# Order of emission: steps of the other small-matmul streams wait for the next step of the RWKV7 recurrence and go right behind it

## The chip, the cores and the metric

The kernel runs on one core of one Trainium2 chip (TensorE, VectorE, ScalarE, GpSimd, and SyncE, which issues most of the DMAs). The metric is the device time of one execution in microseconds (us); the time of a kernel is the median of its runs. In the profile the engines are called PE (matmul), PEld (weight load of the PE), DVE (VectorE), ACT (ScalarE), POOL (GpSimd) and SP (SyncE).

## What is computed

Two blocks of two layers each, on 256 tokens with 1024 features, all in float32. The change lies in the first block. Each of its two layers projects the normed input to 18688 columns and runs three mixers on them:

```python
proj = h @ w_in[l]                                     # 1024 -> 18688, 73 chunks of 256 columns
y_a = hgrn2_mixer(a_q, a_ff, a_fb, a_i, ...) * silu(a_g)    # gated linear recurrence, two directions
y_b = retention_mixer(b_q, b_k, b_v, ...) * silu(b_g)       # retention, two directions
y_c = rwkv7_mixer(c_s, mu, ...) * silu(c_g)                 # RWKV7 recurrence, two directions
mixed = gates[0]*(y_a @ w_branch_a) + gates[1]*(y_b @ w_branch_b) + gates[2]*(y_c @ w_branch_c)
x = x + mixed @ w_out[l]
```

The second block (feed-forward, short convolution, latent attention) follows and is not touched.

## The kernel before

**Large matmuls.** Every dense product is done with three TensorE passes: weight and activation are each split into a high and a low float32r part (`split`, L386 on ScalarE and L387 on VectorE or GpSimd), and `mm3` (L345, L346, L347) multiplies low by high, high by low and high by high, each with 128 x 128 weights and 256 moving columns. A chunk of 256 output columns is 16 such steps, 48 matmuls. Weights come as 512 KB loads from the SP queue into `raw` and are split in halves into `whi` and `wlo`.

**Small matmuls.** The mixers work in float32 on pieces of 32 to 128 rows, in PE tiles written in the profile as 32*32, 64*64, 64*128 or 128*32. The RWKV7 recurrence treats eight pairs of heads one after the other. Its matmuls, all in `rwkv_states`, write `psc` (L967), `pb` (L975), `prv` (L984), `pt` (L992), `pw` and `px` (L1018, L1026, and L1041, L1047), `ch` (L1065, L1072, L1081) and `po` (L1099, L1106). The HGRN2 heads write `ppc` (L1227, L1257), `ppt` (L1265, L1271) and `hpo` (L1181); the retention heads `rps` (L1335) and `rpo` (L1346); the preparation of the recurrence's operands `pv` (L877) and `pl` (L891, L892); column sums and their spreading over a tile stand in helpers (L405, L445, L453).

**Streams.** Inside a layer five Python generators emit this work: `recurrences`, `heads` (four pairs of HGRN2 heads, then four of retention heads), `outs`, `operands`, and `weights`, which emits the large matmuls. A generator runs to its next `yield`. A small stream yields its step's planned TensorE time and the planned time until its next step can start, both in ns; `weights` yields 320 after each three-matmul step; a function that is yielded means "wait until this holds" (mostly an event in `ev`, such as a buffer of the ring of five `hj` tiles having been used). `recurrences` yields gaps of 1000 to 2500, for example

```python
            yield 1740, 1200
            tt(W, pw, C["mw"][:, L].unsqueeze(2).to_broadcast([128, 2, 4, 32]), ALU.mult)
```

and `heads`, for each of five levels of a head, `yield 0, 3000` (elementwise work alone) and `yield 440, 0` (its matmuls).

**What sets the order.** `weave` walks a planned clock. At each turn it takes the first small stream, in the order recurrences, heads, outs, operands, that is due by that clock; if none is, the next step of `weights` goes; if `weights` waits, the earliest of the others goes. The planned gap is stretched by 1.3 for recurrences and outs, 1.35 for heads and 0.8 for operands. So `weave` only decides the order in which instructions are emitted. The framework then places them on each engine by that order and by what is ready, and lets the instructions of the recurrence on VectorE, ScalarE and GpSimd move ahead by a fixed number of places (`Ahead`). No wait of the hardware comes from `weave` itself; an engine executes its queue in order, and waits come from data and from buffers.

When `weights` finds that a ring buffer is not yet free, it first emits other large work that needs none (`spare`: gate chunks of the first two branches, or the next r, k, v, g chunk of the recurrence), and then waits.

Of the kernel before, what the change touches and what calls it, by code (L numbers as in the profile page):

```python
# [19 lines left out]
EC = math.exp(-0.5)  # L20
SH = 20.0
NEG = -1e30
RING, NB = 5, 4


# [13 lines left out]
def weave(chains, fill):  # L39

    scale = dict(chains)
    now, ready, wait, live = 0.0, {}, {}, list(scale) + [fill]
    while live:
        free = []
        for g in live:
            if g in wait and wait[g]():
                del wait[g]
                ready[g] = max(now, ready.get(g, 0.0))  # L50
            if g not in wait:
                free.append(g)
        g = next((g for g in free if g is not fill and ready.get(g, 0.0) <= now), None)
        if g is None:
            g = fill if fill in free else min(free, key=lambda g: ready.get(g, 0.0))
        now = max(now, ready.get(g, 0.0))
        v = next(g, None)
        if v is None:
            live.remove(g)
        elif callable(v):  # L60
            wait[g] = v
        elif g is fill:
            now += v
        else:
            now += v[0]
            ready[g] = now + scale[g] * v[1]


# [93 lines left out]
def consts_second():  # L162
# [7 lines left out]
    i = np.arange(128)  # L170
    caus = np.where(i[:, None] >= i[None, :], 0.0, NEG)
    mask = np.concatenate([caus, np.zeros((128, 128)), caus], 1)
# [324 lines left out]
class First(Core):  # L497
# [73 lines left out]
    def layer(s, l, then):  # L571
# [223 lines left out]
        if l == 0:  # L795
            nc.sync.dma_start(out=s.c1, in_=s.a["c1"])
        weave(((recurrences(), 1.3), (heads(), 1.35), (outs(), 1.3), (operands(), 0.8)), weights())
        run(out_c(0))
        run(out_c(1))
# [1034 lines left out]
```

## Time and profile before

| | us |
|---|---|
| median of 3 runs | 2808.9 |
| lowest and highest run | 2807.0, 2813.6 |
| the profiled execution, whole | 2819.4 |
| its span, first to last instruction | 2817.6 |
| PE busy in the span | 2662.0 (94%) |
| DVE busy in the span | 1946.3 (69%) |

The profiled execution is 10.5 us (0.4%) above the median, and 1.8 us of it lie outside its span. The two layers of the first block run from about 40 to 840 us and from 920 to 1720 us; the second block follows to the end. In a timeline of PE each row is a run of equal instructions with its start and its duration. Large matmuls overlap: a new one starts about every 0.12 us, though each is shown with 0.28 us, so starts are to be compared, not durations.

### The profile page before, as it was taken

What the parts mean: (1) busy time and instruction counts of PE and PEld (TensorE: products, weight loads), DVE (VectorE), ACT (ScalarE), POOL (GpSimd) and SP (SyncE); (2) the same over time, 40 slices, a digit from 0 to 9 for tenths busy, and PEclk for the clock granted to TensorE, in tenths of its full rate; (3) what the DMA queues carried; (4) which work ended last, traced back from release to release, by engine and by line L of the source; (5) the groups of instructions that cost most, each with busy time, mean ns of one, the idle gap of its engine ahead of it and who ended that gap; (6) DMA issues with size and microseconds to landing.
All of it is one profiled execution on the core that took longest, in us unless ns stands there. A gap on an engine that the chain in (4) does not pass through costs nothing.

```text
span 2817.6 us, 76691 instructions
## 1 busy us (share of the span) xinstructions
PE 2662.0 (94%) x32003; PEld 2508.6 (89%) x32003; DVE 1946.3 (69%) x4045; ACT 1488.4 (53%) x2964; POOL 917.1 (33%) x868
## 2 busy tenths in 40 slices
PE   7898999999998899899999999999999999999999
PEld 7788888989998788788888999999899999997999
DVE  7878778776666977789776666755665665665654
ACT  6555555544455655555444445645455555545554
POOL 4333333322344433334233235222222322221222
PEclk9999999999999999999999999999999999998999
DMA  5333332333455333332333345555445554542555
GB/s 175 116 104 102 106 99 84 108 118 110 139 168 176 110 121 106 99 103 80 109 124 112 113 145 183 187 172 184 146 165 183 182 177 165 165 147 67 172 182 163
DMA packets 111804, 385.41 MB, mean 137 GB/s; under 512 B 12384, under 2 KB 16992, under 8 KB 111200
## 3 DMA queue, kind: packets, MB, share of 16 engines
q1 hardware_dynamic: 111024, 379.86, 41.7%
q8 instruction: 251, 4.11, 0.6%
q14 instruction: 97, 0.79, 0.1%
q10 hardware_dynamic: 432, 0.64, 0.1%
HBM read 378.36 MB, written 2.10 MB: 135 GB/s over the span
## 4 chain that ended last, share of the span: by engine, by line
PE 64%; DVE 11%; ACT 4%; issue 4%; POOL 3%; DMA 2%; ACTq 0%; POOLq 0%; DVEq 0%
PE pj L345 5%; PE pj L347 4%; PE pj L346 4%; PE pg L345 3%; PE pg L347 3%; PE pg L346 3%; PE pw L345 3%; PE pw L347 3%; PE pw L346 3%; PE pu L345 3%; PE pu L347 3%; PE pu L346 3%; DVE wlo L387 2%; PE pb L345 2%; PE pb L346 2%
## 5 line engine op out<-in xcount | busy, mean ns | idle before, releaser
L386 ACT CAST whi<-raw 128x512 fp32r<-128x512 f32 (+1 forms) x1407 | 858.4, 617 | 819.9 <-PE pj L347 230.7
L387 POOL TENSOR_TENSOR wlo<-raw,whi 128x512 fp32r<-128x512 f32 (+1 forms) x469 | 632.0, 1348 | 1534.2 <-ACT whi L386 1308.4
L387 DVE TENSOR_TENSOR wlo<-raw,whi 128x512 fp32r<-128x512 f32 x938 | 710.2, 762 | 441.1 <-ACT whi L386 436.2
L345 PE MATMUL pj<-hb,wlo 128*128 128x256 f32 x1408 | 431.5, 307 | 3.9 <-DVE wlo L387 1.6
L346 PE MATMUL pj<-hb,whi 128*128 128x256 f32 x1408 | 406.9, 289 | 0.7 <-DVE hb L387 0.7
L347 PE MATMUL pj<-hb,whi 128*128 128x256 f32 x1408 | 405.3, 288 | 0.6 <-issue 0.6
L345 PEld LDWEIGHTS pj<-hb,wlo 128*128 128x128 f32 x1408 | 273.4, 194 | 17.0 <-DVE wlo L387 1.9
L346 PEld LDWEIGHTS pj<-hb,whi 128*128 128x128 f32 x1408 | 274.2, 195 | 3.1 <-DVE hb L387 1.5
L347 PEld LDWEIGHTS pj<-hb,whi 128*128 128x128 f32 x1408 | 273.8, 195 | 2.0 <-issue 0.8
L345 PE MATMUL pg<-hs,wlo 128*128 128x256 f32 x704 | 200.2, 284 | 1.4 <-DVE x L493 1.1
L345 PE MATMUL pu<-hs,wlo 128*128 128x256 f32 x704 | 201.1, 286 | 0.3 <-POOL wlo L387 0.2
L347 PE MATMUL pu<-hs,whi 128*128 128x256 f32 x704 | 200.6, 285 | 0.0
L346 PE MATMUL pu<-hs,whi 128*128 128x256 f32 x704 | 200.4, 285 | 0.0
L345 PE MATMUL pw<-g,wlo 128*128 128x256 f32 x704 | 199.5, 283 | 0.0
L346 PE MATMUL pg<-hs,whi 128*128 128x256 f32 x704 | 199.5, 283 | 0.0
L347 PE MATMUL pg<-hs,whi 128*128 128x256 f32 x704 | 199.4, 283 | 0.0
L346 PE MATMUL pw<-g,whi 128*128 128x256 f32 x704 | 199.2, 283 | 0.0
L347 PE MATMUL pw<-g,whi 128*128 128x256 f32 x704 | 199.2, 283 | 0.0
L345 PE MATMUL pb<-hs,wlo 128*128 128x256 f32 x512 | 150.3, 293 | 1.6 <-DVE gb L847 1.6
L347 PE MATMUL pb<-hs,whi 128*128 128x256 f32 x512 | 145.0, 283 | 0.0
L346 PE MATMUL pb<-hs,whi 128*128 128x256 f32 x512 | 145.0, 283 | 0.0
L345 PEld LDWEIGHTS pu<-hs,wlo 128*128 128x128 f32 x704 | 136.2, 193 | 1.1 <-POOL wlo L387 0.7
(524 smaller groups left out, 7099.7 us busy)
## 6 DMA issues: line engine op xcount, KB each, us to landing
raw<-in_win SPq DMA_DIRECT2D x292, 512.0 KB, 3.6
raw<-in_w SPq DMA_DIRECT2D x256, 512.0 KB, 3.8
raw<-in_wbb SPq DMA_DIRECT2D x32, 512.0 KB, 3.5
raw<-in_wo SPq DMA_DIRECT2D x32, 512.0 KB, 3.6
raw<-in_wconv SPq DMA_DIRECT2D x20, 512.0 KB, 3.5
raw<-in_wba SPq DMA_DIRECT2D x16, 512.0 KB, 3.5
raw<-in_wbc SPq DMA_DIRECT2D x16, 512.0 KB, 3.7
raw<-in_lora SPq DMA_DIRECT2D x16, 256.0 KB, 2.8
```

What stands on the lines that cost most here:

```text
L345: mm(out=out, lhsT=al, rhs=bh, start=start, stop=False)
L346: mm(out=out, lhsT=ah, rhs=bl, start=False, stop=False)
L347: mm(out=out, lhsT=ah, rhs=bh, start=False, stop=stop)
L386: s.nc.scalar.copy(dh, src)
L387: (eng or s.nc.vector).tensor_tensor(dl, src, dh.bitcast(F32), ALU.subtract)
```

## The change

In `weave`, a step of a small stream other than the first (`lead`, the recurrence) is no longer taken at once when it is due. If no small step with TensorE work has been emitted since the last large step (`small` is false), if `weights` can go and if the recurrence is not waiting for an event and is due within 2000 ns of the planned clock, the large step goes instead. The held step is looked at again at each turn; once a step of the recurrence with TensorE work has been emitted, `small` is true and every due step of the other streams goes right behind it, until the next large step makes `small` false again. Steps without TensorE work are held in the same way. Nothing is computed differently, and no instruction is added or removed.

```diff
+TOGETHER = 2000.0
     now, ready, wait, live = 0.0, {}, {}, list(scale) + [fill]
+    lead, small = chains[0][0], False
     while live:
         ...
         g = next((g for g in free if g is not fill and ready.get(g, 0.0) <= now), None)
+        if (g is not None and g is not lead and not small and fill in free and lead in free
+                and ready.get(lead, 0.0) < now + TOGETHER):
+            g = None
         if g is None:
             g = fill if fill in free else min(free, key=lambda g: ready.get(g, 0.0))
         ...
         elif g is fill:
             now += v
+            small = False
         else:
             now += v[0]
+            small = small or v[0] > 0
             ready[g] = now + scale[g] * v[1]
```

## Rows read from the trace of the kernel before

**Rows 1.** Page, busy time: engine, us, share of the span, instructions.
```profile
PE 2662.0 (94%) x32003; PEld 2508.6 (89%) x32003; DVE 1946.3 (69%) x4045; ACT 1488.4 (53%) x2964; POOL 917.1 (33%) x868
```

**Rows 2.** Windows, the two layers' streams and the second block; columns in the first row.
```profile
core 0: us, PE busy (x) PEld busy (x) DVE busy (x) ACT busy (x) POOL busy (x), PEclk, DMA share, GB/s
40.00:840.00 800.00, 749.56 (x11359) 688.23 (x11358) 605.85 (x1305) 419.37 (x869) 274.27 (x287) 0.97 0.35 114
920.00:1720.00 800.00, 750.15 (x11359) 688.16 (x11358) 608.38 (x1294) 425.65 (x884) 285.15 (x295) 0.97 0.36 114
```

**Rows 3.** PE timeline, a step of the recurrence alone: start, us, line, tiles, count.
```profile
309.27 0.28 PE L346 MATMUL pj<-wlo,hb 128*128 128x256 f32 x1
309.39 0.28 PE L347 MATMUL pj<-whi,hb 128*128 128x256 f32 x1
309.60 0.45 PE L1072 MATMUL ch<-RV,X 64*64 64x64 f32 x8
309.98 0.39 PE L345 MATMUL pj<-whi,hb 128*128 128x256 f32 x1
310.20 0.28 PE L346 MATMUL pj<-wlo,hb 128*128 128x256 f32 x1
310.32 0.28 PE L347 MATMUL pj<-whi,hb 128*128 128x256 f32 x1
```

**Rows 4.** PE timeline, a heads step alone, and the next recurrence step.
```profile
317.79 0.28 PE L347 MATMUL pj<-hb,whi 128*128 128x256 f32 x1
318.00 0.33 PE L1257 MATMUL ppc<-Z 128*32 128x32 f32 x16
318.26 0.39 PE L345 MATMUL pj<-hb,wlo 128*128 128x256 f32 x1
318.48 0.28 PE L346 MATMUL pj<-hb,whi 128*128 128x256 f32 x1
...
318.81 0.45 PE L1081 MATMUL ch<-UV,bT 128*64 128x64 f32 x8
```

**Rows 5.** PE timeline, a heads step right behind a recurrence step.
```profile
323.30 0.28 PE L347 MATMUL pg<-hb,whi 128*128 128x256 f32 x1
323.51 0.45 PE L1072 MATMUL ch<-R,X 64*64 64x64 f32 x8
323.89 0.33 PE L1265 MATMUL ppt<-Z 128*32 128x32 f32 x16
324.15 0.38 PE L345 MATMUL pg<-hb,wlo 128*128 128x256 f32 x1
324.37 0.28 PE L346 MATMUL pg<-hb,whi 128*128 128x256 f32 x1
```

**Rows 6.** PE timeline, first and last of 94 separate steps near a recurrence step.
```profile
91.38 0.39 PE L891 MATMUL pl<-codes,wlo 128*128 128x256 f32 x1 [0.24 <-ACT sg L893]
...
92.39 0.75 PE L1018 MATMUL pw<-XY,SC 32*32 32x32 f32 x64
...
1571.34 1.99 PE L1346 MATMUL rpo<-Pr,sv 128*128 128x256 f32 x8 [0.17 <-DVE sv L1312]
...
1573.50 0.69 PE L1018 MATMUL pw<-XY,SC 32*32 32x32 f32 x58
```

**Rows 7.** Waits of PE, 40 to 840 us: who waited for whom, us, times, longest.
```profile
PE hpo L1181 <- POOL P L1280: 7.2, 4, 3.2
...
PE pn L453 <- DVE SC L80: 4.0, 3, 2.1
...
PE pl L891 <- ACT sg L893: 2.6, 4, 1.9
...
PE ppt L1271 <- DVE Z L1250: 2.5, 1, 2.5
...
PE rps L1335 <- DVE qk L1292: 1.9, 1, 1.9
```

**Rows 8.** Windows, a stretch between two HGRN2 pairs and its neighbours; columns as in rows 2.
```profile
412.00:421.00 9.00, 9.00 (x151) 8.29 (x150) 5.51 (x9) 4.32 (x9) 4.40 (x4) 1.00 0.63 220
...
438.00:461.00 23.00, 17.88 (x545) 15.70 (x544) 22.01 (x42) 9.97 (x20) 12.98 (x13) 0.78 0.17 50
```

**Rows 9.** PE timeline in that stretch, two waits.
```profile
451.00 1.08 PE L1018 MATMUL pw<-XY,SC 32*32 32x32 f32 x64 [2.75 <-DVE XY L80]
453.63 0.58 PE L345 MATMUL pj<-hb,wlo 128*128 128x256 f32 x1 [1.55 <-DVE wlo L387]
```

**Rows 10.** Tiles `po` (end of the recurrence) and `hs`: count, ns min/median/max, first and last start, 40 to 840 us.
```profile
L1106 PE MATMUL po<-ar,S x192: 218/218/267, 154.2 to 748.0; 64*64 64x64 f32 x192
...
L387 DVE TENSOR_TENSOR hs<-yo,hs x4: 682/684/693, 184.9 to 500.6; 128x512 fp32r<-128x512 f32 x4
...
L345 PE MATMUL pb<-hs,wlo x200: 277/283/388, 548.5 to 839.9; 128*128 128x256 f32 x100
```

**Rows 11.** Page, DMA issues: tile, queue, count, KB each, median us to landing.
```profile
raw<-in_win SPq DMA_DIRECT2D x292, 512.0 KB, 3.6
...
raw<-in_lora SPq DMA_DIRECT2D x16, 256.0 KB, 2.8
```

## The prediction

> **What bounds the kernel now.** I read the page first: PE is busy for 94% of the span, DVE for 69% [rows 1]. Then the windows by stage, because a share of the whole hides the stage that is changed. Only the two layers of the first block go through `weave`, and they are alike: of 800 us each, PE is busy about 750 and DVE about 607, at a granted clock of 0.97 of full speed [rows 2]. So in the stage that the change touches PE is the bound: the end comes earlier only if PE has less to do or waits less. The recurrence is not the bound, though it leads the order: its last matmul of the first layer starts at 748.0 us, while large matmuls go on to about 840 us [rows 10]. Next the timeline of PE, row by row: large matmuls start 0.12 us apart, and small steps cut in between them. Here the reader should compare starts. Last, the waits of PE: the ones named ahead of steps of the other streams sum to 18.2 us in the first layer [rows 7], a fiftieth of its 800 us.
>
> **What one bundle saves.** From the last large matmul before a small step to the second one behind it there would be 2 x 0.12 = 0.24 us without the step. With an 8-matmul step of the recurrence alone it is 310.20 - 309.39 = 0.81, so that step costs 0.57 us [rows 3]. A heads step of 16 matmuls alone: 318.48 - 317.79 = 0.69, cost 0.45 [rows 4]. The same kinds one behind the other: 324.37 - 323.30 = 1.07, cost 0.83 [rows 5]. Together they cost 0.57 + 0.45 - 0.83 = 0.19 us less than apart. One sees where it lies: the first small step starts 0.21 instead of 0.12 behind the large matmul, and the second large matmul behind starts 0.22 instead of 0.12 behind the first; a bundle pays each of these once instead of twice. The border inside the bundle is not free: the heads step starts 0.38 us behind the recurrence's [rows 5], as a large matmul does [rows 3].
>
> [...]
>
> **How many bundles.** In the timeline of PE I marked every run of small matmuls between two large ones. In the two stretches 40 to 835 and 920 to 1720 us there are 71 + 71 runs with no matmul of the recurrence in them. The change can move only those that stand shortly ahead of a step of the recurrence. In 47 + 47 = 94 of them the next matmul of the recurrence starts less than 2 us behind their last one's end; first and last are in [rows 6], and the second run of [rows 4] is of this kind (318.00, the recurrence at 318.81). I take 2 us of the trace for 2000 ns of the planned clock, which is rough. By line the 94 are: 34 of the HGRN2 heads (L1227, L1257, L1265, L1271), 8 of the retention heads (L1335, L1346), 25 column sums and spreads (L405, L445, L453), 27 of the operands (L877, L891, L892). The last kind I take as staying: four `pl` products of a pair go through few PSUM buffers and wait for ScalarE to empty them (2.6 us in four waits [rows 7]), so they come apart wherever they are emitted. Of the 25 sums and spreads I take half, since their inputs are a chain of small VectorE operations that may not be done at the moment of the bundle. That is 34 + 8 + 12 = 54 bundles, 54 x 0.19 = **10.3 us less**. Bounds: none forms, 0; all 94 form, 94 x 0.19 = 17.9 us.
>
> **Waits of PE ahead of the moved steps.** A held step comes up to 2 us later, so its inputs are more often there: `hpo` waited 7.2 us for GpSimd in four waits [rows 7]. But PE's queue is in order, and a late input then holds the step behind the recurrence just as well. I take 0; at best half of the 18.2 us in each layer goes, about 18 us in all; at worst the recurrence's own results queue on VectorE behind the elementwise work that now comes with the bundle, priced as the starved stretch below.
>
> **Steps without TensorE work, DMAs, queues.** The elementwise steps of `heads` are held too; they cost nothing by themselves, since VectorE, ScalarE and GpSimd have the same instructions as before and a quarter of VectorE's time is free in the stage [rows 2]. What is queued behind them on VectorE are splits of weights (L387) and the recurrence's own copies, which come sooner. The first step of `operands` issues the load of `lora` on the SP queue; held by up to 2 us it may fall behind one more 512 KB load, that is 3.6 us from issue to landing [rows 11], and the recurrence of the pair before runs for tens of us meanwhile (its ends are (748.0 - 154.2) / 7 = 85 us apart [rows 10]). I take 0 for it, 0 to 4 us per pair if that cover were gone. The change adds no wait of the hardware, so nothing new is queued behind one.
>
> **The delay of `heads`, the cost that the trace does not show.** Each hold makes the chain of heads later against the large matmuls. `weights` needs that chain: the ring of five buffers is freed by it. If large work runs out of buffers and spares, only small steps are emitted, until heads has caught up. Such a stretch stands in the trace of before: 438 to 461 us, where DVE is busy 22.0 of 23 us, PE 17.9, DMA drops from 0.63 to 0.17 and the granted clock is 0.78 [rows 8]. [...] The last output of the HGRN2 heads is split at 500.6 and first used by the branch at 548.5 [rows 10], so the use itself has 48 us of room; the ring has less. About 17 + 17 of the bundles are holds of the HGRN2 heads, each by one to three us, some 35 us by an estimate from these numbers for each layer's chain. I take 0 because the hold is off whenever `weights` waits, so the chain then runs at its old pace; the upper bound is one more such stretch in each layer, 20 us.
>
> [...]
>
> **Sum.** 2819.4 (profiled execution) - 10.3 = 2809.1. That execution lies 10.5 us above the median, so for the median 2808.9 - 10.3 = 2798.6, **2799 us**.
>
> **Rivals.** (1) The bundles don't do what they say: the placement on PE goes by what is ready, and a recurrence step whose VectorE input is late lets the held step or large matmuls go first; or the saving is paid back by waits of a few us in each layer. For it: the 27 `pl` runs come apart already, and PE's waits ahead of recurrence steps are many. Against it: steps that meet today do stand side by side [rows 5]. Fewer than 29 bundles (5.6 us / 0.19) then, or a loss of up to 16 us beside 54: about 2808 us. (2) The other side: **starved stretches.** The held heads come later, `weights` runs against the ring once more in each layer, and VectorE becomes the bound there: 2 x 10 = 20 us, less 10.3 from the bundles, +10 us, 2819 us; with no bundles 2829. It decides from 5 us a layer, half of one such stretch. For it: VectorE is full in that stretch already. Against it: one such stretch in 800 us is all I found in this layer's hgrn part, and the hold is off while `weights` waits. (3) A larger gain: all 94 bundles and half of the waits, 17.9 + 18 = 36 us, 2773 us; it needs everything to go well, and I count it within the first case, with little chance.
>
> **How the numbers follow.** Less than 0.2%, 5.6 us, can hardly be told from no change here. Forecast (faster, 2780 to 2803): 0.43. Rival 1 (within 0.2%): 0.27. Rival 2 (slower): 0.30. The range for 8 in 10 goes down to 54 bundles and the waits' 18 us, 28 us, 2781, and up to rival 2 with hardly any bundles, 2828.
>
> **What would show it.** In the profile after: fewer runs of small matmuls without a recurrence matmul (71 in each stretch before; some 44 after), more heads steps that start 0.3 to 1 us behind `ch`, `pw` or `px` with no large matmul between, PE busy in both windows a little lower at the same clock, and the ends of the streams at about 835 and 1710 us. I am wrong in the bundles if the count of runs stays above 60; wrong in the delay if a window between two HGRN2 pairs shows DVE full, a low DMA share and a clock under 0.9 where before it was 1.0; and wrong in kind if the time moves but the two layers' windows do not, since nothing else is changed.

## The result, and the profile after

The changed kernel takes 2836.1 us (median of 6 runs, 2826.1 to 2840.1) against 2814.1 us for the kernel before on the same chip (6 runs, 2807.0 to 2818.7): a ratio of 1.0074 [1.0057, 1.009]. By that ratio it is slower by 0.74%, 21 us (the two medians lie 22 us apart); the forecast was 10 us less, and 2836 lies above the whole range. Line numbers of the changed kernel are those of the kernel before plus 8 (L345 is L353, L1181 is L1189).

The page of after, busy times (answers [rows 1]): every engine does about what it did, and the span is 2832.5 instead of 2817.6 us. PE stands still for 167.3 us of it instead of 155.6 (span less busy time): 11.7 of the 14.9 us.

```profile
PE 2665.2 (94%) x32003; PEld 2509.8 (89%) x32003; DVE 1949.3 (69%) x4045; ACT 1498.6 (53%) x2970; POOL 909.8 (32%) x868
```

The large matmuls `po` with which each layer ends show where those 14.9 us arise (count, ns, first start, in the first layer, and last start, in the second, in us; before, then after):

```profile
L347 PE MATMUL po<-hb,whi x128: 276/282/283, 863.6 to 1766.9; 128*128 128x256 f32 x128
...
L355 PE MATMUL po<-hb,whi x128: 276/282/415, 870.5 to 1784.6; 128*128 128x256 f32 x128
```

They start 6.9 us later in the first layer and end 17.7 us later in the second; what follows to the end of the span takes 1050.7 and 1047.9 us. The loss lies in the two layers.

Windows of after, the first layer in three parts and the middle of the second layer; the columns are those of [rows 2] (us, busy time of each engine, granted clock, DMA share, GB/s):

```profile
44.00:344.00 300.00, 273.53 (x4370) 250.08 (x4369) 241.31 (x524) 171.71 (x353) 105.83 (x118) 0.97 0.34 106
344.00:544.00 200.00, 178.83 (x3336) 156.17 (x3335) 167.07 (x396) 108.73 (x232) 64.12 (x77) 0.96 0.28 86
544.00:840.00 296.00, 287.95 (x3561) 272.34 (x3561) 192.45 (x376) 135.70 (x275) 98.23 (x90) 0.99 0.42 134
...
1220.00:1420.00 200.00, 180.52 (x3419) 157.66 (x3417) 169.58 (x396) 114.72 (x242) 68.06 (x81) 0.96 0.26 81
```

The same windows of the kernel before:

```profile
44.00:344.00 300.00, 269.01 (x4317) 244.56 (x4316) 249.11 (x531) 173.19 (x355) 110.00 (x123) 0.97 0.33 108
344.00:544.00 200.00, 186.85 (x3347) 167.55 (x3346) 158.26 (x381) 102.99 (x219) 63.56 (x72) 0.95 0.29 92
544.00:840.00 296.00, 289.70 (x3667) 272.11 (x3667) 195.00 (x387) 141.15 (x292) 100.71 (x92) 0.99 0.41 133
...
1220.00:1420.00 200.00, 186.97 (x3406) 167.60 (x3405) 169.34 (x395) 108.64 (x235) 65.80 (x80) 0.98 0.30 95
```

The rows say where PE is less busy. Up to 344 us the change is ahead: PE is busy 4.5 us more, DVE 7.8 us less. Then, in the 200 us in which the second half of the HGRN2 heads lies, PE is busy 8.0 us less and DVE 8.8 us more; the second layer repeats it with 6.5 us less of PE. Over the whole of 40 to 840 us the difference is 5.2 us (749.6 in [rows 2], 744.3 after), which shows neither.

Inside those 200 us, windows of 10 us of after in which PE is busy less than 8.5 us:

```profile
374.00:384.00 10.00, 7.52 (x76) 5.61 (x75) 5.91 (x13) 2.73 (x7) 5.10 (x6) 0.66 0.26 79
...
424.00:434.00 10.00, 5.76 (x220) 5.00 (x218) 10.00 (x17) 6.57 (x12) 5.89 (x7) 0.99 0.01 3
434.00:444.00 10.00, 8.19 (x226) 7.38 (x227) 9.05 (x16) 4.31 (x9) 3.24 (x3) 0.84 0.70 213
...
464.00:474.00 10.00, 8.04 (x62) 6.62 (x62) 6.86 (x15) 3.33 (x7) 5.73 (x7) 0.87 0.26 79
...
524.00:534.00 10.00, 7.83 (x61) 6.95 (x62) 8.33 (x15) 4.28 (x11) 4.24 (x4) 0.83 0.39 113
```

There are five. In the kernel before there are two, one of them the starved stretch of [rows 8]:

```profile
394.00:404.00 10.00, 7.78 (x78) 6.71 (x77) 8.95 (x22) 8.58 (x15) 5.60 (x5) 1.00 0.18 55
...
444.00:454.00 10.00, 5.09 (x205) 4.22 (x204) 9.56 (x16) 3.49 (x7) 8.53 (x10) 0.79 0.02 3
```

The PE timeline of after in the worst of its five (start, duration, instruction, and in brackets the wait ahead of it and who ended it; answers [rows 9]):

```profile
429.81 0.28 PE L353 MATMUL pj<-whi,hb 128*128 128x256 f32 x1
432.65 0.74 PE L1026 MATMUL pw<-XY,SC 32*32 32x32 f32 x64 [2.56 <-DVE XY L88]
433.93 0.58 PE L353 MATMUL pj<-hb,wlo 128*128 128x256 f32 x1 [0.54 <-DVE wlo L395]
434.31 0.41 PE L354 MATMUL pj<-hb,whi 128*128 128x256 f32 x1
434.53 0.41 PE L355 MATMUL pj<-hb,whi 128*128 128x256 f32 x1
434.74 0.41 PE L353 MATMUL pj<-hb,wlo 128*128 128x256 f32 x1
434.95 0.41 PE L354 MATMUL pj<-hb,whi 128*128 128x256 f32 x1
```

And what VectorE was doing meanwhile: groups of after between 424 and 434 us (count, busy us, mean ns).

```profile
L395 DVE TENSOR_TENSOR wlo<-raw,whi 128x512 fp32r<-128x512 f32 x2 | 2.9, 1486 | 0.0
...
L926 DVE SCALAR_TENSOR_TENSOR bt<-sg,nkk 128x512 f32<-128x512 f32 x1 | 1.7, 1743 | 0.0
...
L1225 DVE TENSOR_TENSOR D<-S 128x512 f32<-128x512 f32 x1 | 1.1, 1123 | 0.0
...
L88 DVE STREAM_TRANSPOSE XY<-XY 128x256 f32<-128x256 f32 x2 | 0.9, 432 | 0.0
```

The recurrence waits 2.56 us for a transpose of 0.43 us. VectorE is full for 10.00 of the 10 us: between the `px` that the recurrence's next step needs (PE, 428.68 us) and that transpose (432.07 us) it does operands (L926 for 1.74 us, L932 for 0.68 us), and in the same window the next heads (L1225, 1.1 us) and weight splits (L395, 2.9 us); for one of these splits the large matmul at 433.93 us waits another 0.54 us. Behind the waits the large matmuls start 0.21 to 0.22 us apart one after the other, where [rows 3] has 0.12; the granted clock of their window, 434 to 444 us, is 0.84. This is no loss of the whole layer, though: from 40 to 840 us the granted clock is 0.97 in both kernels.

Tiles of after: the output of the HGRN2 heads (`hpo`, with its row of before first), its split (`hs`), the branch that uses it (`pb`), and the recurrence's last matmul (count, ns, first and last start in us; answers [rows 10]):

```profile
L1181 PE MATMUL hpo<-P,v x32: 378/379/794, 120.2 to 489.4; 128*128 128x256 f32 x32
...
L1189 PE MATMUL hpo<-P,v x32: 377/379/797, 136.2 to 528.2; 128*128 128x256 f32 x32
...
L395 DVE TENSOR_TENSOR hs<-yo,hs x4: 659/676/691, 208.8 to 542.0; 128x512 fp32r<-128x512 f32 x4
...
L353 PE MATMUL pb<-hs,wlo x236: 274/283/418, 564.6 to 859.7; 128*128 128x256 f32 x118
...
L1114 PE MATMUL po<-ar,S x192: 218/218/267, 154.3 to 719.1; 64*64 64x64 f32 x192
```

The last output of the heads comes at 528.2 instead of 489.4 us, their last split at 542.0 instead of 500.6 us, and the branch's first use at 564.6 instead of 548.5. The recurrence, for whose sake heads was held, ends at 719.1 instead of 748.0: 29 us earlier, and the layer ends later all the same.

Last, a bundle of after. It is formed as intended (compare [rows 5]): no large matmul between, the second small step 0.38 us behind the first.

```profile
122.07 0.28 PE L355 MATMUL pj<-hb,whi 128*128 128x256 f32 x1
122.28 0.45 PE L1049 MATMUL pw<-XY,SC 32*32 32x32 f32 x32
122.66 0.45 PE L1279 MATMUL ppt<-Z 128*64 128x64 f32 x8
123.05 0.39 PE L353 MATMUL pg<-hb,wlo 128*128 128x256 f32 x1
```

Runs of small matmuls with no recurrence matmul in them: 56 and 55 in the two layers, 71 and 71 before (counted in the PE timeline).

### The profile page after: what moved, and what is told of

It reads as the page before. It is cut to its first block, busy times and chain, and to the rows that moved or that the text cites. A ratio compares the mean times of both kernels' runs of the same rounds, so it can differ in the third digit from the quotient of the medians.

```text
span 2832.5 us, 76727 instructions
## 1 busy us (share of the span) xinstructions
PE 2665.2 (94%) x32003; PEld 2509.8 (89%) x32003; DVE 1949.3 (69%) x4045; ACT 1498.6 (53%) x2970; POOL 909.8 (32%) x868
## 5 line engine op out<-in xcount | busy, mean ns | idle before, releaser
L395 POOL TENSOR_TENSOR wlo<-raw,whi 128x512 fp32r<-128x512 f32 (+1 forms) x469 | 628.2, 1340 | 1524.8 <-ACT whi L394 1319.3
L395 DVE TENSOR_TENSOR wlo<-raw,whi 128x512 fp32r<-128x512 f32 x938 | 716.3, 769 | 459.9 <-ACT whi L394 453.8
L353 PE MATMUL pj<-hb,wlo 128*128 128x256 f32 x1408 | 430.1, 306 | 6.5 <-DVE wlo L395 5.2
L353 PEld LDWEIGHTS pj<-hb,wlo 128*128 128x128 f32 x1408 | 275.4, 196 | 17.9 <-DVE wlo L395 5.4
L353 PE MATMUL pg<-hs,wlo 128*128 128x256 f32 x704 | 200.2, 284 | 3.1 <-DVE wlo L395 1.9
L353 PE MATMUL pu<-hs,wlo 128*128 128x256 f32 x704 | 199.9, 284 | 0.4 <-POOL wlo L395 0.3
L353 PE MATMUL pw<-g,wlo 128*128 128x256 f32 x704 | 199.7, 284 | 0.1
L353 PE MATMUL pb<-hs,wlo 128*128 128x256 f32 x512 | 147.6, 288 | 6.6 <-DVE gr L828 5.0
L353 PEld LDWEIGHTS pg<-hs,wlo 128*128 128x128 f32 x704 | 134.9, 192 | 4.0 <-DVE wlo L395 2.4
```

The source lines that it names most:

```text
L353: mm(out=out, lhsT=al, rhs=bh, start=start, stop=False)
L395: (eng or s.nc.vector).tensor_tensor(dl, src, dh.bitcast(F32), ALU.subtract)
```

## The experiments

The change does three things at once: it delays heads, it puts held steps behind the recurrence's step instead of ahead of it, and it joins them into one run. The theory to test: the delay of heads is the whole loss. The rivals: the bundle itself is bad (the recurrence's results queue behind the joined elementwise work), or the hold of the other two streams is.

Some expectations use the planned clock of `weave`: follow its turns over the generators' yields, adding them as the code does, and note when the fourth pair of HGRN2 heads ends, counted from the layer's start. This is 400 us for the kernel before and 459 us after the change; `weights` finds itself waiting for 40 and 86 us of it. It is no time of the chip, only a measure of the order. No experiment leaves out or changes any of the computation. "hpo" in the table is the last start of that tile in the two layers of the profiled execution, "PE" the busy time of PE in 344 to 544 us; both are of one execution, the ratios are of all. What follows the second layer's large matmuls, which no run changes, took between 1040 and 1058 us in these executions, so a few us between two of them say little.

| kernel | hold | pace of heads | ratio to before [95%] | hpo, us | PE, us |
|---|---|---|---|---|---|
| before | none | 1.35 | 1 | 489, 1361 | 186.9 |
| after | bundled | 1.35 | 1.0074 [1.0057, 1.009] | 528, 1416 | 178.8 |
| e9, after again | bundled | 1.35 | 1.0055 [1.0035, 1.0075] | 522, 1407 | 180.1 |
| e13, after again | bundled | 1.35 | 1.0074 [1.0048, 1.0099] | 523, 1414 | 178.7 |
| e1 | none | 1.55 | 1.0044 [1.0024, 1.0064] | 526, 1417 | 176.5 |
| e15 | none | 1.6 | 1.0078 [1.0063, 1.0094] | 534, 1427 | 178.5 |
| e11 | heads alone | 1.35 | 1.0084 [1.0065, 1.0103] | 535, 1425 | 178.9 |
| e4 | all but heads | 1.35 | 0.997 [0.9956, 0.9984] | 476, 1355 | 184.8 |
| e6 | bundled | 1.05 | 0.9979 [0.9965, 0.9992] | 477, 1354 | 187.6 |
| e2 | bundled | 1.0 | 0.995 [0.993, 0.9969] | 470, 1348 | 186.2 |
| e8 | bundled | 0.95 | 0.9949 [0.9929, 0.9969] | 448, 1323 | 185.9 |
| e12 | bundled | 0.9 | 1.0056 [1.0041, 1.007] | 429, 1317 | 186.7 |
| e7 | none | 1.2 | 1.0019 [1.0002, 1.0036] | 456, 1337 | 187.0 |
| e3 | none | 1.0 | 1.0111 [1.0088, 1.0135] | 409, 1300 | 187.9 |
| e5 | held, apart | 1.35 | 1.0034 [1.002, 1.0047] | 532, 1411 | 178.3 |
| e14, e5 again | held, apart | 1.35 | 1.0028 [1.0015, 1.0041] | 530, 1416 | 178.9 |
| e16 | held, apart | 1.05 | 0.9963 [0.9944, 0.9982] | 481, 1354 | 187.4 |
| e10 | held, apart | 0.95 | 0.9944 [0.9929, 0.9959] | 454, 1329 | 191.0 |

### The delay without the hold, and the hold without the delay

e1 is the kernel before with heads slowed by hand; e2 is the changed kernel with heads sped up so that the hold's delay is made good:

```diff
 e1 (before):  - (heads(), 1.35)   + (heads(), 1.55)
 e2 (after):   - (heads(), 1.35)   + (heads(), 1.0)
```

> The kernel before, without the hold; only the planned gap of heads is stretched by 1.55 instead of 1.35. By the planned clock the fourth HGRN2 pair then ends at 457 us of its layer, as in the changed kernel (459; before 400), while separate runs of small matmuls stay as many as before. Theory A (the change costs because it delays heads, so that the large matmuls run out of ring buffers): slower than before by 0.5 to 1%, as the change, about 15 to 25 us. Theory B (the bundles themselves cost, by long stretches of small matmuls and a lower clock): within 0.2% of before.

> The changed kernel, hold and bundles kept; the planned gap of heads is stretched by 1.0 instead of 1.35, so that by the planned clock the fourth HGRN2 pair ends at 368 us (changed 459, before 400) and the large matmuls never wait for the ring. Theory A: the loss is gone, 2795 to 2815 us, and separate runs without the recurrence stay near 55 a layer. Theory B: still 0.5 to 1% slower than before, about 2830 us. Either way PE may wait more ahead of heads steps, since they are emitted closer together: by up to 10 us a layer.

Measured: e1 1.0044 [1.0024, 1.0064], e2 0.995 [0.993, 0.9969]. The delay alone loses, and without the delay the change gains. In e1 the same 200 us of the first layer lose PE work as in after, with no hold in the kernel:

```profile
344.00:544.00 200.00, 176.53 (x3109) 155.20 (x3110) 164.11 (x374) 103.14 (x226) 60.08 (x74) 0.92 0.27 82
```

e1 lost less than the change, so part of the loss might still have been the hold's. e15 delays a little more, in one set with e13, the change once more:

```diff
 e15 (before): - (heads(), 1.35)   + (heads(), 1.6)
```

> The kernel before, no hold, heads stretched by 1.6: fourth HGRN2 pair at 461 us by the planned clock, large work waits 84 us (changed: 459 and 86). The delay alone, matched more closely than with 1.55. Delay theory: as the change, 1.004 to 1.007. If the hold has a cost of its own: at most 1.003.

> The changed kernel, beside e14 and e15. Delay theory: the three agree within their intervals, all at 1.004 to 1.007. If bundles under a delay cost by themselves: this one is 0.2% or more above both others.

e15 1.0078 [1.0063, 1.0094], e13 1.0074 [1.0048, 1.0099]: a delay with no hold costs as much as the change. Between 1.55 and 1.6 the planned end moves by only 4 us (457 to 461) and the cost by 0.34%; the two come from different sets and their intervals just meet (1.0063 to 1.0064), so this may be chance, or the planned end does not say everything about an order.

### Which stream's hold

```diff
 e4 (after):   - g is not lead and not small   + g is not lead and g is not chains[1][0] and not small
 e11 (after):  - g is not lead and not small   + g is chains[1][0] and not small
```

> The changed kernel, but heads is never held; outs and operands still are. Theory A: within 0.2% of before, about 2814 us, since nobody waits for these two in time (by the planned clock the fourth HGRN2 pair ends at 391 us, before 400). Theory B: a third of the loss at most, since a third of the held steps are theirs: 2814 to 2821 us.

> The changed kernel, but only heads is held; outs and operands are not. By the planned clock the fourth HGRN2 pair ends at 459 us, as in the change. Theory A: the same loss as the change, 0.5 to 1.0%, since holding outs and operands alone made the kernel 0.3% faster. If the loss needs all three held: within 0.3% of before.

e4, where heads is never held, 0.997 [0.9956, 0.9984]; e11, where only heads is, 1.0084 [1.0065, 1.0103]. The hold of `outs` and `operands` costs nothing (e4 is 0.3% faster than before, a little more than its expectation of within 0.2%); that of `heads` is all of the loss. The tile's row of e11 against that of e4 shows the delay, 60 us at the end of the first layer's heads. e11:

```profile
L1189 PE MATMUL hpo<-P,v x32: 377/379/793, 134.9 to 535.0; 128*128 128x256 f32 x32
```

e4:

```profile
L1189 PE MATMUL hpo<-P,v x32: 377/379/793, 120.6 to 475.5; 128*128 128x256 f32 x32
```

### Is it the pace alone?

If early heads were simply better, the kernel before would gain by it without any hold. e3 and e7 change the pace of before; e6, e8 and e12 that of after.

```diff
 e3, e7 (before):      - (heads(), 1.35)   + (heads(), 1.0), + (heads(), 1.2)
 e6, e8, e12 (after):  - (heads(), 1.35)   + (heads(), 1.05), + (heads(), 0.95), + (heads(), 0.9)
```

> The kernel before, without the hold, heads stretched by 1.0: the control of the run before it. By the planned clock the fourth HGRN2 pair ends at 302 us. What it differs by from that run is the price or the profit of hold and bundles where heads is not late. Theory A with bundles that pay 0.19 us each: the run with the hold is 3 to 10 us faster than this one. Theory B: it is 10 to 20 us slower. Against before itself: within 0.4%, since PE has the same work.

> The kernel before, no hold, heads stretched by 1.2: by the planned clock the fourth HGRN2 pair ends at 350 us and the large matmuls never wait for the ring, as in the run with hold and 1.0 (368, no waits). It says what of that run's gain of 0.5% is pace alone. Theory A with bundles that pay: between before and that run or a little slower than before by waits for heads' data, 2805 to 2825 us. If the gain is pace alone: 2800 to 2808 us.

> The changed kernel with heads stretched by 1.05: by the planned clock the fourth HGRN2 pair ends at 396 us and the large matmuls wait 37 us, as before (400 and 40), and planned runs without the recurrence are 19 a layer instead of 41. So this is hold and bundles at the old pace of heads. Theory A with bundles that pay: 8 to 12 us faster than before, as forecast for the change itself. If they pay nothing: within 0.2% of before. Theory B: still slower than before by 0.4% or more.

> The changed kernel with heads stretched by 0.95: fourth HGRN2 pair at 356 us by the planned clock, no ring waits, 16 planned runs without the recurrence. A neighbour of the fastest run so far: within 0.3% of it, 2796 to 2812 us, if pace between 356 and 368 us does not matter; slower by more if heads' steps now come ahead of their data.

> The changed kernel with heads stretched by 0.9: fourth HGRN2 pair at 324 us by the planned clock. Without the hold, going from 350 to 302 us cost 0.9%, by waits of PE ahead of heads steps. If the hold keeps heads' steps behind their data: within 0.2% of the run at 0.95, 0.4 to 0.7% faster than before. If pace below 350 us costs whatever the hold: 0.3% or more slower than the run at 0.95.

Without the hold, early heads lose: e7 1.0019 [1.0002, 1.0036], e3 1.0111 [1.0088, 1.0135], the worst of all. With the hold, heads may come earlier and gain: e6 0.9979 [0.9965, 0.9992], e8 0.9949 [0.9929, 0.9969]; at e12 that is overdone, 1.0056 [1.0041, 1.007]. So the pace has an optimum, and the two sides look different in the traces. Late heads lose PE time in 344 to 544 us: 176.5 to 180.1 us in all eight executions that end hpo behind 520 us (five kernels, one of them three times and one twice), 184.8 to 191.0 in the others. That loss is not yet the kernel's loss. e5 and e14 of the next part have late heads too and lose the same 8 us in the window, but over the whole of 40 to 840 us PE does not fall behind in them (749.6 before; after, e5, e14):

```profile
40.00:840.00 800.00, 744.31 (x11297) 682.59 (x11296) 604.83 (x1301) 418.45 (x865) 269.68 (x285) 0.97 0.36 112
...
40.00:840.00 800.00, 751.45 (x11348) 688.66 (x11347) 608.70 (x1304) 419.80 (x871) 275.33 (x287) 0.98 0.36 114
...
40.00:840.00 800.00, 753.08 (x11358) 690.86 (x11357) 608.71 (x1305) 420.91 (x871) 275.46 (x287) 0.97 0.36 114
```

In e3 the window from 344 us is full, and PE waits more ahead of steps of the other streams: of heads, 23.2 us in the first layer against 14.0 before, and of `outs` (`pn`). Some of its rows of waits (40 to 860 us; us, times, longest; [rows 7] has 7.2 for `hpo` and 4.0 for `pn`):

```profile
PE hpo L1181 <- POOL P L1280: 9.6, 5, 3.0
...
PE pn L453 <- DVE SC L80: 9.0, 5, 3.1
...
PE ppc L1257 <- DVE Z L1250: 3.4, 4, 1.7
...
PE ppt L1271 <- DVE Z L1250: 2.9, 2, 2.1
```

### Does the bundle pay?

e5 keeps the hold but not the bundle: a held step goes one large step behind the recurrence's step, so a large step stands between the two. Held steps that go in the same gap between two large steps still stand together.

```diff
-    lead, small = chains[0][0], False
+    lead, small = chains[0][0], 0
-        if g is not None and g is not lead and not small and fill in free and lead in free and (...)
+        if (g is not None and g is not lead and small != 2 and fill in free
+                and (small == 1 or lead in free and ready.get(lead, 0.0) < now + TOGETHER)):
         elif g is fill:
-            small = False
+            small = 2 if small == 1 else 0
         else:
-            small = small or v[0] > 0
+            if g is lead and v[0] > 0: small = 1
```

> The changed kernel's holds without its bundles: a held step waits for the next step of the recurrence and then for one more large step, so it stands alone behind that. By the planned clock the fourth HGRN2 pair ends at 464 us (changed 459) and the large matmuls wait 88 us for the ring (86), so the delay is the same; planned separate runs without the recurrence are 70 a layer instead of 18. Theory A, with bundles that pay 0.19 us: slower than the changed kernel by about 50 x 2 x 0.19 = 19 us, so 1.2 to 1.5% slower than before. If bundles pay nothing: as the changed kernel, 0.5 to 0.9% slower than before. Theory B (bundles cost): faster than the changed kernel.

> The changed kernel once more, beside the others of this set. Slower than before by 0.5 to 0.9%, about 2830 to 2842 us for a before of 2816 us. If it comes out near 0.4%, the delay of heads alone (heads stretched by 1.55: 0.44% slower) is the whole loss; if at 0.7% or above, bundling under that delay adds to it.

> The hold without bundles, heads stretched by 1.35 (fourth HGRN2 pair at 464 us by the planned clock). Delay theory: as the change, 1.004 to 1.007. If bundles cost: 1.002 to 1.004, below the change. If bundles pay 0.19 us each: 1.010 or more.

e5 1.0034 [1.002, 1.0047] and e14 1.0028 [1.0015, 1.0041] against after's 1.0074, 1.0055 and 1.0074: with the delay, apart is no worse than together but better, by 0.2 to 0.45%; e13 and e14, of one set, are separated by their intervals. By the expectation of e14 this is the case in which bundles cost, so the rival is half right: with heads equally late (hpo 522 to 534 us), the delay without a hold (e15) costs 0.78%, with the hold bundled 0.55 to 0.74%, with the hold apart 0.3%. The delay is the loss; the hold apart wins more than half of it back, and bundled little or nothing. At the two paces without the delay the two forms cannot be told apart:

```diff
 e16 (e5): - (heads(), 1.35)   + (heads(), 1.05)
 e10 (e5): - (heads(), 1.35)   + (heads(), 0.95)
```

> The hold without bundles, heads stretched by 1.05: fourth HGRN2 pair at 396 us by the planned clock, as before (400) and as the hold with bundles at 1.05 (396; 0.9979). If bundles pay 0.19 us: 0.5% above that one, 1.002 to 1.004. If they pay nothing: 0.996 to 0.9995.

> Hold without bundles at the fast pace: a held step stands alone behind the large step that follows the recurrence's, and heads is stretched by 0.95. By the planned clock the fourth HGRN2 pair ends at 357 us with no ring waits, as with bundles at 0.95 (356, none; 0.5% faster than before); planned runs without the recurrence are 94 a layer instead of 16. If a bundle pays the 0.19 us of the trace: 35 to 40 more runs of small matmuls in the trace, 14 to 16 us slower than with bundles, so within 0.2% of before. If bundles pay nothing: 0.5% faster than before, as with bundles. If the bundles' clock costs: faster still.

e16 0.9963 [0.9944, 0.9982] beside e6's 0.9979; e10 **0.9944 [0.9929, 0.9959]**, 2799.9 us, beside e8's 0.9949. e10 has the lowest ratio found (e2 and e8 lie inside its interval) and beats both kernels of this study, yet it has 107 and 109 runs of small matmuls without the recurrence, where e8 has 51 and 56 and the kernel before 71 and 71. Its pairs of steps stand apart, as in its PE timeline:

```profile
123.16 0.45 PE L1050 MATMUL pw<-XY,SC 32*32 32x32 f32 x32 [0.77 <-DVE XY L89]
123.54 0.39 PE L354 MATMUL pj<-hb,wlo 128*128 128x256 f32 x1
123.76 0.28 PE L355 MATMUL pj<-hb,whi 128*128 128x256 f32 x1
123.88 0.28 PE L356 MATMUL pj<-hb,whi 128*128 128x256 f32 x1
124.09 0.46 PE L1236 MATMUL ppc<-D,EK 128*32 128x32 f32 x32
```

and the 200 us in which after loses PE time are the fullest of all:

```profile
344.00:544.00 200.00, 190.95 (x3118) 172.73 (x3118) 159.14 (x353) 106.92 (x223) 67.46 (x72) 0.97 0.34 106
```

## Why the prediction was wrong

**What bounds the kernel: right.** The loss lies in the two layers (6.9 us later at the end of the first, 17.7 at the end of the second), and PE lacks its time in the same stretch of both.

**What one bundle saves, and how many: formed, but mis-sized and not paid.** The runs without the recurrence fell by 15 + 16 = 31, not by 54, which at 0.19 us would be 5.9 us. That saving was read rightly from [rows 3 to 5], but it is the saving of a pattern, not of the kernel: e10 and e8 differ by 56 + 53 = 109 such runs, 20 us at 0.19 each, and by nothing in time that their intervals show. Their pages say where it goes (e8, then e10; spans 2803.5 and 2806.2 us):

```profile
PE 2645.4 (94%) x32003; PEld 2496.7 (89%) x32003; DVE 1956.1 (70%) x4045; ACT 1493.3 (53%) x2970; POOL 913.0 (33%) x868
...
PE 2660.0 (95%) x32003; PEld 2503.1 (89%) x32003; DVE 1957.9 (70%) x4045; ACT 1496.8 (53%) x2972; POOL 914.1 (33%) x868
```

PE is busy 14.6 us less in e8, most of the 20 (a part of it may be the granted clock, 0.979 and 0.977); but it stands still, span less busy time, for 158.1 us in e8 and 146.2 in e10, and that takes 11.9 us back. A large step between two small ones, three starts 0.12 us apart [rows 3], is by estimate 0.36 us of cover for VectorE's answer, and a bundle gives that cover up; this is an argument, and no run measured it by itself. From the start of a step of 8 small matmuls to the next start it is 0.38 us, whether a small step comes next [rows 5] or a large matmul [rows 3], and the ratios of e10 and e8 (0.9944, 0.9949) show that fewer changes between small and large matmuls need not give time.

**Waits ahead of the moved steps: taken as 0, and they rose.** The 18.2 us were the rows that [rows 7] shows; all waits ahead of the other streams' steps are 23.4 us in 40 to 840 us and 25.7 in 920 to 1720. The change lowered them to 18.8 and 18.5, 11.8 us in all. That a late input holds what stands behind it in PE's queue is seen in the trace of before: ahead of `ch` (L1081, 402.36 us) PE stands still 1.83 us for VectorE, and L346 of the product whose L345 started at 400.25 us comes only behind it, at 402.74. But the waits ahead of the recurrence's own steps rose from 44.7 to 53.8 us in the two stretches and those ahead of large matmuls from 5.2 to 15.6, 19.5 us in all. The prediction's worst case, the recurrence's results queueing on VectorE, did come, but not by the bundle alone: ahead of the recurrence's steps e5, with steps apart, has 54.7 us, and of the two kernels that are only delayed e15 has 52.3 and e1 43.9; ahead of large matmuls those two have 5.0 and 11.4. One execution of each does not part the hold from the delay. Where heads is early enough, the hold does gain: at nearly the same planned end of heads (350 and 356 us), the hold is worth 0.7% (e7 1.0019, e8 0.9949); at the pace of before, 0.2 to 0.4% (e6, e16, against 1). The PE's waits ahead of steps of the other streams, summed over the timeline, are 29.7 and 33.2 us in e7 and 16.7 and 22.2 in e10. So at the pace of before the hold is worth 6 to 10 us, between the prediction's 0 and its upper bound of 18. The kernels with the hold have in common that a step comes behind the recurrence's step rather than just ahead of it; that this place is what pays is read from them, no run tests it by itself.

**The delay of heads: the step that failed.** The prediction had the mechanism, named the ring, estimated some 35 us for each layer's chain, and then took 0 "because the hold is off whenever `weights` waits, so the chain then runs at its old pace". The delay was 39 us in the first layer (hpo 489 to 528) and 55 in the second (1361 to 1416), 7 of which are the later start of that layer; the 35 us were a fair estimate, the price of 0 was not. The reason for 0 was wrong: the hold being off while `weights` waits stops the delay from growing, but makes nothing good, and from there on a delay costs: a delay alone, e15, 0.78%, about 22 us, and the hold without the delay gains up to 0.5%. The stated place of the loss, windows between two HGRN2 pairs, was right; its form, one more starved stretch of 10 us a layer, only in part. After has one stretch in which DVE is full, DMA almost none and PE short by over 4 us (424 to 434 us), as before has (444 to 454), and no second one; the rest of PE's lack is spread over the other windows below 8.5 us.

**Sizes.** The loss of the change is 16 to 21 us over three sets (1.0055 to 1.0074). Rival 2 gave 20 us lost less 10.3 from bundles, 2819; what was wrong in it was the credit. Without bundles it gave 2829, near the measured 2836 and below it, and what it needed, one more starved stretch in each layer, is not what the trace shows. Of its 10 us a stretch, on which the upper end of the range rests too, [rows 8] show 5.1 us, 23 less 17.9 of PE; the other 5 no run shows. In their place the trace of before has, behind the waits of [rows 9], 16 large matmuls between 454 and 460 us that start 0.21 to 0.22 us apart instead of 0.12, and two steps of 64 small matmuls that take 1.08 instead of 0.75 us [rows 6]: by estimate 16 x 0.09 + 2 x 0.33 = 2.1 us. The chance of 0.30 was put on the rival of whose price half stood in the rows, and 0.43 on a gain for which the whole working went by single patterns; the upper end, 2828, had no room for a delay in both layers that costs more than one stretch each.

**The tests named.** Runs below 60: met, so the bundles are not where it failed. A window between two HGRN2 pairs with DVE full, little DMA and a low clock: 424 to 444 us, where the first half has DVE 10.00 and DMA 0.01, and the clock falls in the second, 0.84; the kernel before has such a stretch 20 us later, so the test shows a stretch that moved rather than one that was added.

**What stays open.** That the delay of heads is the loss is shown by slowing heads alone and by taking the delay out. How a delay costs is not. That late heads cost PE time in 344 to 544 us stands in eight executions of five kernels, but two of them make it good within the first layer (e5, e14); and the loss has no one form: in after PE stands still 11.7 us longer than before and is busy 3.2 us longer, in e15 it stands still 5.7 us longer and is busy 15.1 us longer (2677.1 us, at a granted clock of 0.974 against 0.977). That VectorE work of heads falls together with the next pair's operands and the weight splits is read from one stretch of one trace (424 to 434 us) and from DVE's 8.8 us more in that window; a larger ring, which would part the ring's share from VectorE's, was not tried.

## What to carry to other kernels

When independent streams are interleaved by hand, a rule that lets one stream go first moves the others' phase; work out how late each ends and what waits for it before counting what the rule saves at a step, and set the stream's pace anew with the rule (here 1.35 to 0.95 turned +0.74% into -0.5%). A saving read from one pattern of the timeline is an upper bound until a kernel that has the pattern and one that has not have been timed at the same pace: joining small steps was worth nothing at the fast pace and cost 0.2 to 0.45% at the slow one, and the rule that places them behind the recurrence's step, joined or not, was worth up to 0.7%.

## What the runs showed that was not expected

Heads that end too early lose as heads that end too late do: with no hold, hpo ending at 409 us costs 1.11%, at 534 us 0.78%, both against 489 us. And the kernel with most changes between small and large tiles (e10, 107 and 109 runs of small matmuls outside the recurrence) has the lowest ratio, with the fullest PE in the stretch where the change loses PE time: 191.0 of 200 us.
